# Six RMS norms of a hybrid decoder block: the factors computed per position on VectorE instead of per column with ScalarE's tables

## The chip, the cores and the metric

The kernel runs on one core of a Trainium2 chip. The time is device microseconds (us) of one execution of the whole program, weights and activations starting in device memory. A core has five engines, each with its own in-order queue of instructions: TensorE (PE in the profile, with its weight loads as PEld), VectorE (DVE), ScalarE (ACT), GpSimd (POOL) and SyncE (SP). Engines wait for one another only through semaphores, so an instruction that waits also holds back everything behind it on its own engine.

## The reference, cut to what matters

One decoder layer in float32 on 2048 positions with 1024 channels: a norm, two token mixers side by side, an output projection with a residual, a second norm, a SwiGLU feed-forward with a residual, and a final norm.

```python
def rmsnorm(x, g):
    y = x * lax.rsqrt(jnp.mean(x * x, axis=-1, keepdims=True) + 1e-6)
    return y * g

h = rmsnorm(x, norm1_g)
proj = h @ w_in                      # both mixers' inputs
o_gla = ...                          # chunked gated linear attention, per-head norm, gate
o_conv = c_b * causal_depthwise_conv(c_c * c_h, conv_w)
x = x + jnp.concatenate([o_gla, o_conv], -1) @ w_out
h2 = rmsnorm(x, norm2_g)             # rewritten by the change
x = x + (silu(h2 @ w_ffn_gate) * (h2 @ w_ffn_up)) @ w_ffn_down   # 1024 -> 2816 -> 1024
return rmsnorm(x, norm_f_g)          # rewritten for the first half of the positions
```

The quantity in question is the factor `rsqrt(mean(x*x) + eps)`: one number for each position, shared by its 1024 channels.

## The kernel before, in words

**Layout.** The positions are cut into four blocks of 512 (`PB`), and two blocks form a half. A block is held transposed: 128 channels on the partitions and 512 positions along the free axis, in `KD` = 8 such tiles for the 1024 channels. A norm therefore has to add over the partitions, and its factor has to be the same on all 128 partitions of a column.

**Products.** Every float32 operand is split into a high and a low part (`split`: L145 copies it on ScalarE with rounding, L146 subtracts on VectorE), and each product runs as three matmuls (`product_step`, L358, L359 and L360). A `unit` multiplies a 2x2 arrangement of tiles with seven products in place of eight, so it needs sums and differences of weights (L341 to L348 on GpSimd, the splits giving tiles `wq`) and collects results with a copy on ScalarE (L378) and adds on VectorE (L382, tile `c`). `out_proj` uses plain products (L776, L777, L779) in four groups for pairs of output tiles; each group ends with four adds `y<-y,mm` on VectorE (L801), a store and squares that go into `ssx0` and `ssx1`, the running sums of squares of the two blocks of a half (ScalarE squares, GpSimd adds).

**Stages.** Projections and mixers come first, until 600.1 us in the trace. Then `out_proj(0)` and `out_proj(1)` run, then for each half `ffn_up` (11 rounds of two units, the second multiplied in at L876) and `ffn_down`.

**The norms.** There are six that the change touches, two in each of three generators:
- `h2_first` (L807) makes the first half's normed operands while TensorE does `out_proj(1)`. It calls `column_rstd` (L159 on, its sum at L163) for each of its two blocks with a factor in SBUF, tile `rb2`, and then goes into `combine`, whose scalings `h<-h,sml,rb` are L482 on VectorE.
- `h2_ahead` (L846) makes the second half's operands while `ffn_up(0)` runs, with `psum_rstd` (sum at L170) and a factor in PSUM.
- `finish_later` (L949) does the final norm of the first half while the feed-forward of the second half runs: it loads the first half's result tile by tile (`y`), squares it, calls `psum_rstd`, loads the tiles again, scales them and stores them to the output (L965). It first calls `preload_act_table_set`.

In all of them `ones` (128x128) times the 128x512 sum of squares puts the total on every partition; `finish_rstd` (L173 on) then takes logarithm and exponential on ScalarE (L176, L177, each with its own table set where another function came in between), the mean on VectorE (L178) and one Newton step of three operations (`newton`, L154 to L157). The final norm of the second half, in `last_unit` (L968 on), calls `finish_rstd` itself.

**What sets the order.** The generators yield after each small step. `out_proj` takes steps of `h2_first` itself; elsewhere `tick()`, called after each product, steps the queue `background` on every second call and the generator in `ahead` on every fourth. The resulting program is then ordered on each engine by a planner (`TileContext` with `schedule_with_timeline_sim=True`), which estimates when each instruction can start. All transfers are issued by SyncE's queue. PSUM's eight banks are one pool (`ps`), from which totals, factors and products take theirs in turn.

Of the kernel before, what the change touches and what calls it, by code (L numbers as in the profile page):

```python
# [10 lines left out]
F32 = mybir.dt.float32  # L11
F32R = mybir.dt.float32r
U32 = mybir.dt.uint32
AF = mybir.ActivationFunctionType
ALU = mybir.AluOpType
PSUM = bass.MemoryType.PSUM
# [2 lines left out]
P = 128  # L19
D = 1024  # L20
# [4 lines left out]
PT = PB // P  # L25
# [5 lines left out]
EPS = 1e-6  # L31
# [16 lines left out]
def tile_hymba_block(ctx, tc, x, xt, win, wa, wgu, wout, wffn, wdown, wdown_first, small, out):  # L48
    nc = tc.nc
    act, dve, pool, pe = nc.scalar, nc.vector, nc.gpsimd, nc.tensor  # L50

    def pool_of(name, bufs, **kw):
        return ctx.enter_context(tc.tile_pool(name=name, bufs=bufs, **kw))

    const = pool_of("const", 1)
# [4 lines left out]
    tiny = pool_of("tiny", 2)  # L60
# [4 lines left out]
    mixer = mixing.enter_context(tc.tile_pool(name="mixer", bufs=1))  # L65
# [1 line left out]
    bx = [mixing.enter_context(tc.tile_pool(name="bx", bufs=11)), None]  # L67


    ident = mixer.tile([P, P], F32, name="ident")  # L70
    make_identity(nc, ident)
    ones = const.tile([P, P], F32, name="ones")
    dve.memset(ones[:], 1.0)
# [6 lines left out]
    one_t = ones[:, 0:1]  # L80
# [43 lines left out]
    def col(c):  # L124
        return sml[:, c : c + 1]

    def bank(name="mm"):
        return ps.tile([P, PB], F32, name=name, tag="mm")

    def tt(name):  # L130
        return tp.tile([P, PB], F32, name=name, tag="t")

    def bt(name, shape=(P, PB)):
        return bx[0].tile(list(shape), F32, name=name, tag="b")

    def load(dst, src):
        return nc.sync.dma_start(dst, src)

    def store(dst, src):
        return nc.sync.dma_start(dst, src)  # L140
# [3 lines left out]
    def split(src, hi, lo):  # L144
        last_hi[:] = [act.activation(hi, src, AF.Copy)]  # L145
        return dve.tensor_tensor(lo, src, hi.bitcast(F32), ALU.subtract)  # L146

    def rsqrt(y, v, l, y0):

        act.activation(l, v, AF.Ln)  # L150
        act.activation(y0, l, AF.Exp, scale=-0.5)
        newton(y, v, l, y0)

    def newton(y, v, l, y0):  # L154
        dve.tensor_tensor(l, y0, y0, ALU.mult)
        dve.scalar_tensor_tensor(l, l, -0.5, v, ALU.mult, ALU.mult)
        dve.scalar_tensor_tensor(y, l, 1.5, y0, ALU.add, ALU.mult)  # L157

    def column_rstd(ssq, n, rb=None):  # L159

        rb = ssq if rb is None else rb
        tot = bank("tot")
        pe.matmul(tot[:], ones[:], ssq[:], start=True, stop=True)  # L163
        finish_rstd(rb, tot, n)
        return rb

    def psum_rstd(ssq, n):

        tot, rb = bank("tot"), bank("rb_ps")
        pe.matmul(tot[:], ones[:], ssq[:], start=True, stop=True)  # L170
        finish_rstd(ssq, tot, n, rb)
        return rb

    def finish_rstd(v, tot, n, rb=None):
        l, y0 = bt("l"), bt("y0")
        act.activation(l[:], tot[:], AF.Ln, bias=eps[:], scale=1.0 / n)  # L176
        act.activation(y0[:], l[:], AF.Exp, scale=-0.5)  # L177
        dve.tensor_scalar(v[:], tot[:], 1.0 / n, EPS, ALU.mult, ALU.add)  # L178
        newton((v if rb is None else rb)[:], v[:], l[:], y0[:])
# [33 lines left out]
    def split_op(src):  # L213
        o = opp.tile([P, 2, PB], F32R, name="op", tag="op")
        split(src, o[:, 0, :], o[:, 1, :])
        return o
# [4 lines left out]
    def combine(src, g, rb, put):  # L221


        order = [kj for k in range(4) for kj in ((k, 0), (k, 1), (k + 4, 1), (k + 4, 0))]
        ahead = deque()

        def fetch():
            if order:
                k, j = order.pop(0)
                h = bt("h")  # L230
                load(h[:], src(k, j))
                ahead.append((k, j, h))

        def quad():
            k, j, h = ahead.popleft()
            fetch()
            return scaled(col(g + k), rb[j], h)

        fetch()
        fetch()  # L240
        for k in range(4):
            b11 = quad()
            put("B11", k, b11)
            yield
            b12, t1 = quad(), bt("t1")
            pool.tensor_tensor(t1[:], b12[:], b11[:], ALU.subtract)
            put("T1", k, t1)
            yield
            b22 = quad()
            pool.tensor_tensor(t1[:], b22[:], t1[:], ALU.subtract)  # L250
            put("T2", k, t1)
            yield
            pool.tensor_tensor(b12[:], b22[:], b12[:], ALU.subtract)
            put("T3", k, b12)
            yield
            b21 = quad()
            put("B21", k, b21)
            yield
            pool.tensor_tensor(t1[:], b21[:], t1[:], ALU.subtract)
            put("T4", k, t1)  # L260
            yield
            put("B22", k, b22)
            yield
# [98 lines left out]
    def unit(src, ops, into=None):  # L362
# [13 lines left out]
        def copied(name, o, at):  # L376
            t = tt(name) if into is None else into[at]
            act.activation(t[:], o[:], AF.Copy)  # L378
            return t
# [291 lines left out]
    def gla_scores(b, t, kq, kt, v, g):  # L671
# [6 lines left out]
        for e in range(2):  # L678
            dve.copy_predicated(smv[:, e], mask[:].bitcast(U32), sc[e][:])
        kt_ps = ps.tile([P, 2, P], F32, name="kt_ps", tag="mm")  # L680
# [71 lines left out]
    def sum_squares(ssq, y, first):  # L752
        if first:
            act.activation(ssq[:], y, AF.Square)
        else:
            q = tt("q")
            act.activation(q[:], y, AF.Square)  # L757
            pool.tensor_tensor(ssq[:], ssq[:], q[:], ALU.add)  # L758

    def build_mix(half):  # L760
        def pair(b, k):
            return load_pair(s_gla[b][:, k] if k < HEADS else s_mix[b][k - HEADS])

        return [[pair(2 * half + j, k) for j in range(2)] for k in range(KD)]
# [42 lines left out]
    def h2_first(ssq, ops):  # L807


        for _ in range(6):  # L810
            yield
        rb = []
        for j in range(2):
            rb.append(tiny.tile([P, PB], F32, name="rb2", tag="rb"))
            column_rstd(ssq[j], D, rb[j])
            yield

        def put(n, k, h):
            if n in LATER:
                store(s_h2[n][k][:], h[:])  # L820
            else:
                ops[n].append(split_op(h[:]))

        yield from combine(lambda k, j: s_x1[j][k][:], C_G2, rb, put)

    def h2_rest(ops):
        hs = deque()
        order = [(n, k) for n in LATER for k in range(4)]

        def fetch():  # L830
            if order:
                n, k = order.pop(0)
                h = bt("h")
                load(h[:], s_h2[n][k][:])
                hs.append((n, h))

        for _ in range(4):
            fetch()
        while hs:
            for _ in range(2):  # L840
                n, h = hs.popleft()
                ops[n].append(split_op(h[:]))
                fetch()
            yield

    def h2_ahead(ssq):  # L846


        rb = []
        for j in range(2):  # L850
            for _ in range(2):
                yield
            rb.append(psum_rstd(ssq[j], D))

        def put(n, k, h):
            store_split(s_h2p[n][k], h)

        yield from combine(lambda k, j: s_x1[2 + j][k][:], C_G2, rb, put)
# [34 lines left out]
    def store_split(dst, y):  # L893
        o = bx[1].tile([P, 2, PB], F32R, name="so", tag="so")
        split(y[:], o[:, 0, :], o[:, 1, :])
        store(dst[:], o[:].bitcast(F32))
# [6 lines left out]
    def ffn_down(half):  # L903
# [42 lines left out]
        if half == 0:  # L946
            ahead[:] = [finish_later(half)]

    def finish_later(half):  # L949

        for j in range(2):
            ssq = tiny.tile([P, PB], F32, name="ssx0", tag="ssx0", bufs=1)
            for d in range(KD):
                y = bt("y")
                load(y[:], s_x1[2 * half + j][d][:])
                yield
                sum_squares(ssq, y[:], d == 0)
            yield
            act.preload_act_table_set("natural_log_exp_and_others")
            rb = psum_rstd(ssq, D)  # L960
            for d in range(KD):
                y = bt("y")
                load(y[:], s_x1[2 * half + j][d][:])
                yield
                dve.scalar_tensor_tensor(y[:], y[:], col(C_GF + d), rb[:], ALU.mult, ALU.mult)  # L965
                store(out[2 * half + j, :, d, :], y[:])
# [73 lines left out]
    ssq = out_proj(0, build_mix(0))  # L1040
    drain_background(lambda: (3, PT - 1) in done)
    h2 = no_operands()
    ssq = out_proj(1, build_mix(1), h2_first(ssq, h2), h2_rest(h2))
    ahead.append(h2_ahead(ssq))
    mixing.close()
    bx[:] = [
# [112 lines left out]
```

## Time and profile before

| | |
|---|---|
| median of 3 runs | 2129.43 us (2121.35 to 2132.37) |
| profiled execution | 2130.55 us, span 2128.8 us |
| granted TensorE clock, mean | 0.987 |
| TensorE busy | 2043.5 us (96%), 9133 matmuls |
| VectorE busy | 1415.6 us (66%), 1983 instructions |
| ScalarE busy | 1015.7 us (48%), 1997 instructions |
| GpSimd busy | 971.7 us (46%), 703 instructions |
| DMA | 470.74 MB, 60.6% of 16 engines' time |

In the lines quoted below, a timeline row gives the start in us, the duration in us, the engine, the line of the kernel, the operation, the output and inputs by the program's names, the tile and the count; a row may stand for a few equal instructions in a row (x2, x4). A bracket at the end is the idle time of that engine just before the instruction, and what ended it. A row by groups gives the busy time of the group in us, the mean duration of one in ns, and the idle time before its instructions. A row by stretch gives the stretch, and then busy times with the number of instructions for PE, PEld, DVE, ACT and POOL, the granted clock, the DMA share and the traffic in GB/s.

### The profile page before, as it was taken

How to read it: one execution, taken by the hardware profiler on the slowest of the kernel's cores; microseconds unless marked ns; L12 is line 12 of the kernel's file. 1: busy time of each engine (PE TensorE's matmuls, PEld its weight loads, DVE VectorE, ACT ScalarE, POOL GpSimd, SP SyncE). 2: the span in 40 equal slices, each digit the busy share in tenths (PEclk: the TensorE clock that was granted, in tenths of full speed). 3: DMA queues.
4: the chain of work that ended last, by engine and by line, in shares of the span. 5: the costliest groups of instructions: out<-in, count | busy, mean ns of one | idle time of the engine just before them, and what ended most of it. 6: DMA issues, size and time to landing. Idle time of an engine off the chain costs nothing.

```text
span 2128.8 us, 26931 instructions
## 1 busy us (share of the span) xinstructions
PE 2043.5 (96%) x9133; PEld 1653.7 (78%) x9133; DVE 1415.6 (66%) x1983; ACT 1015.7 (48%) x1997; POOL 971.7 (46%) x703
## 2 busy tenths in 40 slices
PE   5999999999999999999999999999999989999996
PEld 4777787887888888788888877787888878886774
DVE  7668765549753695887886655654766666664554
ACT  5555445656543345545545443333554454453344
POOL 3435322222102464565464437864545545435774
PEclk9999999999999999999999999999999999999998
DMA  7349586424586872655646677697454535587662
GB/s 272 127 149 310 189 337 216 144 100 133 183 302 219 333 275 99 238 198 212 224 168 217 256 304 262 239 343 291 158 211 170 208 129 187 203 330 268 266 267 109
DMA packets 190971, 470.74 MB, mean 221 GB/s; under 512 B 20016, under 2 KB 65264, under 8 KB 181232
## 3 DMA queue, kind: packets, MB, share of 16 engines
q1 hardware_dynamic: 190832, 469.01, 60.6%
q8 instruction: 72, 1.18, 0.2%
q14 instruction: 67, 0.55, 0.1%
HBM read 300.63 MB, written 168.30 MB: 220 GB/s over the span
## 4 chain that ended last, share of the span: by engine, by line
PE 76%; DMA 10%; DVE 8%; ACT 3%; issue 2%; POOL 0%; SPq 0%; DVEq 0%; ACTq 0%; POOLq 0%
PE mm L358 22%; PE mm L360 22%; PE mm L359 21%; PE mm L776 2%; PE mm L777 2%; PE mm L779 2%; DMA raw<-in_wdown_dram 2%; DVE wq L146 2%; DMA op<-sa_T 1%; DMA op<-sa_B 1%; DMA op<-shT 1%; DVE so L146 1%; DVE op L146 1%; DMA h<-in_xt_dram 1%; DVE h L482 1%
## 5 line engine op out<-in xcount | busy, mean ns | idle before, releaser
L358 PE MATMUL mm<-op,wq 128*128 128x512 f32 x2499 | 985.4, 396 | 29.1 <-ACT c L378 9.8
L360 PE MATMUL mm<-op,wq 128*128 128x512 f32 x2499 | 970.4, 393 | 14.9 <-DVE wq L146 14.0
L359 PE MATMUL mm<-op,wq 128*128 128x512 f32 x2499 | 979.2, 392 | 0.0
L146 DVE TENSOR_TENSOR wq<-raw,wq 128x512 fp32r<-128x512 f32 (+2 forms) x626 | 524.6, 844 | 334.0 <-ACT wq L145 332.1
L145 ACT ACTIVATE wq<-raw 128x512 fp32r<-128x512 f32 (+2 forms) x626 | 364.8, 587 | 588.3 <-PE mm L360 421.2
L358 PEld LDWEIGHTS mm<-op,wq 128*128 128x128 f32 x2499 | 472.5, 189 | 147.8 <-ACT c L378 13.1
L360 PEld LDWEIGHTS mm<-op,wq 128*128 128x128 f32 x2499 | 472.5, 189 | 126.5 <-DVE wq L146 27.1
L359 PEld LDWEIGHTS mm<-op,wq 128*128 128x128 f32 x2499 | 472.9, 189 | 97.0 <-issue 1.0
L343 POOL TENSOR_TENSOR raw<-s,raw 128x512 f32<-128x512 f32 (+2 forms) x97 | 127.2, 1311 | 437.2 <-DVE wq L146 416.6
L382 DVE TENSOR_TENSOR c<-mm,c 128x512 f32<-128x512 f32 x267 | 182.8, 685 | 113.2 <-PE mm L360 109.9
L341 POOL TENSOR_TENSOR s<-raw 128x512 f32<-128x512 f32 (+2 forms) x97 | 127.3, 1313 | 196.5 <-DMA raw<-in_wffn_dram 90.3
L348 POOL TENSOR_TENSOR raw<-raw 128x512 f32<-128x512 f32 (+2 forms) x97 | 125.9, 1298 | 137.0 <-DVE wq L146 129.8
L378 ACT ACTIVATE c<-mm 128x512 f32<-128x512 f32 x267 | 154.4, 584 | 26.4 <-PE mm L360 23.9
L758 POOL TENSOR_TENSOR ssx<-ssx,q 128x512 f32<-128x512 f32 x52 | 76.2, 1477 | 159.8 <-ACT q L757 159.6
L342 POOL TENSOR_TENSOR raw<-raw 128x512 f32<-128x512 f32 (+2 forms) x97 | 136.8, 1411 | 4.4
L938 POOL TENSOR_TENSOR y<-c,y 128x512 f32<-128x512 f32 x66 | 99.1, 1504 | 68.9 <-DVE c L382 68.7
L146 DVE TENSOR_TENSOR so<-t,so 128x512 fp32r<-128x512 f32 x100 | 90.8, 914 | 19.0 <-ACT so L145 18.7
L145 ACT ACTIVATE wq<-s 128x512 fp32r<-128x512 f32 (+2 forms) x97 | 56.8, 586 | 92.7 <-PE mm L360 90.7
L776 PE MATMUL mm<-op,wq 128*128 128x512 f32 x256 | 100.9, 395 | 0.0
L777 PE MATMUL mm<-op,wq 128*128 128x512 f32 x256 | 99.8, 390 | 0.0
L146 DVE TENSOR_TENSOR wq<-s,wq 128x512 fp32r<-128x512 f32 (+2 forms) x97 | 86.1, 887 | 16.0 <-ACT wq L145 15.3
L145 ACT ACTIVATE so<-t 128x512 fp32r<-128x512 f32 x100 | 62.5, 628 | 44.2 <-DMA sa_B<-so 17.5
(175 smaller groups left out, 1882.2 us busy)
## 6 DMA issues: line engine op xcount, KB each, us to landing
raw<-in_wffn_dram SPq DMA_DIRECT2D x44, 1024.0 KB, 5.9
sa_T<-so SPq DMA_DIRECT2D x88, 512.0 KB, 5.0
op<-sa_T SPq DMA_DIRECT2D x88, 512.0 KB, 9.6
sa_B<-so SPq DMA_DIRECT2D x69, 512.0 KB, 3.4
op<-sa_B SPq DMA_DIRECT2D x69, 512.0 KB, 9.6
raw<-in_win_dram SPq DMA_DIRECT2D x23, 1024.0 KB, 5.3
raw<-in_wdown_dram SPq DMA_DIRECT2D x24, 768.0 KB, 6.1
sx<-y SPq DMA_DIRECT2D x48, 256.0 KB, 3.1
```

The source lines that it names most:

```text
L145: last_hi[:] = [act.activation(hi, src, AF.Copy)]
L146: return dve.tensor_tensor(lo, src, hi.bitcast(F32), ALU.subtract)
L341: pool.tensor_tensor(s1, a21, a22, ALU.add)
L342: pool.tensor_tensor(a21, a11, a21, ALU.subtract)
L343: pool.tensor_tensor(a11, s1, a11, ALU.subtract)
L358: pe.matmul(o[:], wh, xh, start=first and k == 0, stop=False, skip_group_check=True)
L359: pe.matmul(o[:], wh, xl, start=False, stop=False, skip_group_check=True)
L360: return pe.matmul(o[:], wl, xh, start=False, stop=k == n - 1, skip_group_check=True)
L378: act.activation(t[:], o[:], AF.Copy)
L382: dve.tensor_tensor(t[:], o[:], t[:], ALU.add)
L776: pe.matmul(o[e, j][:], wh, m[:, 0, :], start=k == 0, stop=False)
L777: pe.matmul(o[e, j][:], wh, m[:, 1, :], start=False, stop=False)
```

## The change

`column_rstd` and `psum_rstd` are replaced by `position_rstd`, in all three generators. The sum over partitions is now four matmuls with the 128x128 pieces of the sum of squares as weights and one column of ones as the moving operand. This puts the 512 totals into a 128x4 tile, positions on the partitions, in a PSUM bank `rs`. VectorE computes mean plus epsilon, takes a first guess of the reciprocal root by integer arithmetic on the bits of the number, and improves it in three Newton rounds of three operations, all on 128x4. It then copies each number along 128 columns into `rep` (128x4x128), and four transpositions on TensorE with `ident` put the factors, equal on all partitions, into the PSUM bank `rb_ps`. `h2_first` copies that to SBUF on ScalarE; the other two use it where it is. `ident` moves to a pool that lives to the end of the program, and `finish_later` no longer preloads a table set. `last_unit` is not changed.

```diff
--- before.py
+++ after.py
@@ -11,6 +11,7 @@
 F32 = mybir.dt.float32
 F32R = mybir.dt.float32r
 U32 = mybir.dt.uint32
+I32 = mybir.dt.int32
 AF = mybir.ActivationFunctionType
 ALU = mybir.AluOpType
 PSUM = bass.MemoryType.PSUM
@@ -67,7 +68,7 @@
     bx = [mixing.enter_context(tc.tile_pool(name="bx", bufs=11)), None]
 
 
-    ident = mixer.tile([P, P], F32, name="ident")
+    ident = const.tile([P, P], F32, name="ident")
     make_identity(nc, ident)
     ones = const.tile([P, P], F32, name="ones")
     dve.memset(ones[:], 1.0)
@@ -156,19 +157,29 @@
         dve.scalar_tensor_tensor(l, l, -0.5, v, ALU.mult, ALU.mult)
         dve.scalar_tensor_tensor(y, l, 1.5, y0, ALU.add, ALU.mult)
 
-    def column_rstd(ssq, n, rb=None):
-
-        rb = ssq if rb is None else rb
-        tot = bank("tot")
-        pe.matmul(tot[:], ones[:], ssq[:], start=True, stop=True)
-        finish_rstd(rb, tot, n)
-        return rb
-
-    def psum_rstd(ssq, n):
-
-        tot, rb = bank("tot"), bank("rb_ps")
-        pe.matmul(tot[:], ones[:], ssq[:], start=True, stop=True)
-        finish_rstd(ssq, tot, n, rb)
+    def position_rstd(ssq, n):
+
+
+
+        s, rb = bank("rs"), bank("rb_ps")
+        tot, v, l = [s[:, i * PT : (i + 1) * PT] for i in range(3)]
+        y = tiny.tile([P, PT], F32, name="py", tag="py")[:]
+        for t in range(PT):
+            pe.matmul(
+                tot[:, t : t + 1], ssq[:, t * P : (t + 1) * P], one_t, start=True, stop=True
+            )
+        dve.tensor_scalar(v, tot, 1.0 / n, EPS, ALU.mult, ALU.add)
+        li = l.bitcast(I32)
+        dve.tensor_scalar(li, v.bitcast(I32), 1, None, ALU.arith_shift_right)
+        dve.tensor_scalar(y.bitcast(I32), li, -1, 0x5F3759DF, ALU.mult, ALU.add)
+        for _ in range(3):
+            dve.tensor_tensor(l, v, y, ALU.mult)
+            dve.scalar_tensor_tensor(l, l, -0.5, y, ALU.mult, ALU.mult)
+            dve.scalar_tensor_tensor(y, l, 1.5, y, ALU.add, ALU.mult)
+        rep = bt("rep", (P, PT, P))
+        dve.tensor_copy(rep[:], y.rearrange("p (t c) -> p t c", c=1).to_broadcast([P, PT, P]))
+        for t in range(PT):
+            pe.transpose(rb[:, t * P : (t + 1) * P], rep[:, t, :], ident[:])
         return rb
 
     def finish_rstd(v, tot, n, rb=None):
@@ -812,7 +823,7 @@
         rb = []
         for j in range(2):
             rb.append(tiny.tile([P, PB], F32, name="rb2", tag="rb"))
-            column_rstd(ssq[j], D, rb[j])
+            act.activation(rb[j][:], position_rstd(ssq[j], D)[:], AF.Copy)
             yield
 
         def put(n, k, h):
@@ -850,7 +861,7 @@
         for j in range(2):
             for _ in range(2):
                 yield
-            rb.append(psum_rstd(ssq[j], D))
+            rb.append(position_rstd(ssq[j], D))
 
         def put(n, k, h):
             store_split(s_h2p[n][k], h)
@@ -956,8 +967,7 @@
                 yield
                 sum_squares(ssq, y[:], d == 0)
             yield
-            act.preload_act_table_set("natural_log_exp_and_others")
-            rb = psum_rstd(ssq, D)
+            rb = position_rstd(ssq, D)
             for d in range(KD):
                 y = bt("y")
                 load(y[:], s_x1[2 * half + j][d][:])
```

## The prediction

> **What bounds the kernel now.** I read the page's shares and its chain first, then the waits of TensorE, then the timeline around each of the six norms that the change rewrites.
>
> ```profile
> span 2128.8 us, 26931 instructions
> PE 2043.5 (96%) x9133; PEld 1653.7 (78%) x9133; DVE 1415.6 (66%) x1983; ACT 1015.7 (48%) x1997; POOL 971.7 (46%) x703
> PE 76%; DMA 10%; DVE 8%; ACT 3%; issue 2%; POOL 0%; SPq 0%; DVEq 0%; ACTq 0%; POOLq 0%
> PE mm L360 <- DVE wq L146: 14.0, 11, 2.5
> PE mm L358 <- DVE c L382: 7.7, 2, 7.0
> ```
>
> TensorE is busy for 96% of the span. A change can therefore move the time in three ways: through TensorE's own instructions, through waits that it puts into TensorE's in-order queue, or through waits that it removes. The two wait rows (total, times, longest) name the only large one in the feed-forward: 7.0 us behind one VectorE add. The profiled execution took 2130.55 us, 1.1 above the median of 2129.43; the sum below is made against 2130.55.
>
> **What ScalarE gives up.** In the built program the table loads fall from 29 to 17, and six Ln and six Exp go.
>
> ```profile
> L176 ACT ACT_TABLE_LOAD x4 | 5.1, 1283 | 0.1
> L176 ACT ACTIVATE l<-tot,eps 128x512 f32<-128x512 f32 x8 | 5.5, 684 | 1.6 <-PE tot L984 1.4 <-PE tot L163 0.2
> ```
>
> The 12 loads are 15.4 us and the pairs of activations 7.9 us, on an engine that is busy 48% of the time. By themselves they are worth nothing; they count only where VectorE or TensorE stood behind them.
>
> **TensorE's own instructions.** Each norm loses one product with `ones` over 512 columns and gains four over one column and four transpositions.
>
> ```profile
> 820.40 0.39 PE L360 MATMUL mm<-op,wq 128*128 128x512 f32 x1
> 820.62 1.02 PE L170 MATMUL tot<-ssx,ones 128*128 128x512 f32 x2
> 821.71 0.39 PE L359 MATMUL mm<-op,wq 128*128 128x512 f32 x1
> 387.49 0.39 PE L702 MATMUL o_ps<-carry,kq 128*128 128x128 f32 x2
> 387.71 0.39 PE L700 MATMUL o_ps<-vt,scores 128*128 128x128 f32 x2
> 362.28 0.60 PE L736 MATMUL ot<-ident,osb 128*128 128x128 f32 x4
> 362.95 0.39 PE L359 MATMUL mm<-op,wq 128*128 128x512 f32 x1
> ```
>
> Products start every 0.227 us (the first and last of the rows 715.03 to 725.72 further down are 47 products apart: 10.69 / 47). With the old sum away, L359 at 821.71 would follow the sum's place one step behind 820.62, at 820.85: the sum costs 0.86. Without the four transpositions L358 would start at 362.28 and L359 at 362.51; L359 starts at 362.95, so four cost 0.44. A one-column product in f32 is not in the trace. Its ends are 0.11 (one transposition) and 0.43 (half of the old sum). I take 0.22, the step between two f32 products of 128 columns (387.49 to 387.71), because with so few columns the loading of 128x128 weights sets the step. Four are 0.88. A norm costs 0.88 + 0.44 - 0.86 = +0.46 us, six cost **+2.8** (bounds +0.1 to +7.8).
>
> **VectorE's chain.** Twelve operations on 128x4 that wait for one another and a copy to 128x512 take the place of four operations on 128x512.
>
> ```profile
> 310.98 0.16 DVE L156 SCALAR_TENSOR_TENSOR hl<-hl,hsq 128x4 f32<-128x4 f32 x1
> 311.18 0.16 DVE L157 SCALAR_TENSOR_TENSOR hsq<-hl,hy 128x4 f32<-128x4 f32 x1
> 107.33 0.22 DVE L449 COPY rep<-msq 128x128 f32<-128x128 f32 x1
> 326.50 1.29 POOL L341 TENSOR_TENSOR s<-raw 128x512 f32<-128x512 f32 x1
> 326.94 0.87 DVE L155 TENSOR_TENSOR hl<-hy 128x4 f32<-128x4 f32 x1
> L876 DVE TENSOR_TENSOR c<-c,c 128x512 f32<-128x512 f32 x66 | 69.0, 1045 | 0.0
> L876 DVE TENSOR_TENSOR sg<-mm,sg 128x512 f32<-128x512 f32 x22 | 15.2, 691 | 55.6 <-PE mm L360 55.6
> ```
>
> A step is 0.20 us, so twelve take 2.4. The copy lies between 0.22 (128 columns) and 0.88 (four times that); I take 0.45. The chain is 2.85 us, about what four operations at 0.6 took. The last four rows show a hazard: the 128x4 operation at 326.94 lasts until GpSimd's add ends (327.79). The L876 rows show the same multiplication at 1045 ns with both inputs in SBUF and at 691 ns with one in PSUM. The new steps keep one operand in the PSUM tile `rs`, so I count no such holding for them, only for the copy. The Trainium skill (SBUF — State Buffer, section Who interferes with whom) says that a VectorE instruction with two SBUF inputs contends with GpSimd for an exclusive port pair, and one with a single SBUF input outside the two-port modes does not; by that rule, too, the steps run free, while a copy in a two-port mode can be held. If the steps were held after all, the sum would be the slower rival's.
>
> **The second norm in the second half's `out_proj`.** Here the built order matters. TensorE's queue has the sums of block 0, 37 products, four transpositions, the sums of block 1, the last 11 products of the first group, and then the transpositions of block 1. VectorE's queue has, inside the chain of block 1, the four adds `y<-y,mm` (L801) of that group, the last of which needs its last product, and one weight split behind them. The transpositions thus cannot start before the group's end plus all of that.
>
> ```profile
> 700.87 2.64 DVE L801 TENSOR_TENSOR y<-y,mm 128x512 f32<-128x512 f32 x4 [2.49 <-PE mm L779]
> 713.08 1.88 PE L163 MATMUL tot<-ssx,ones 128*128 128x512 f32 x4
> 715.03 0.39 PE L777 MATMUL mm<-op,wq 128*128 128x512 f32 x1
> 719.86 1.41 DVE L482 SCALAR_TENSOR_TENSOR h<-h,sml,rb 128x512 f32<-128x512 f32 x2
> 725.72 0.39 PE L776 MATMUL mm<-op,wq 128*128 128x512 f32 x1
> 861.58 0.50 PE L360 MATMUL mm<-op,wq 128*128 128x512 f32 x1 [2.51 <-DVE wq L146]
> 861.92 0.40 PE L358 MATMUL mm<-op,wq 128*128 128x512 f32 x1
> 1740.76 0.80 PE L358 MATMUL mm<-op,wq 128*128 128x512 f32 x1 [7.05 <-DVE c L382]
> 1744.31 0.40 PE L360 MATMUL mm<-op,wq 128*128 128x512 f32 x1
> ```
>
> Counted from the group's end (the next group's first product, 725.72 now, some 726.2 then): second add done at +0.3, two further adds 1.3, three steps between 0.6, the split 0.65, four steps 0.8, the copy 0.45, hand-over 0.3: TensorE idles about 4.4 us where it idled none (bounds 3.5 to 7). Slow products follow: after the 7.05 us wait eight of them take 3.55 us instead of 1.82, after the 2.51 us wait none is slow; I take 1.1 between 0 and 1.7. **+5.5**. The Trainium skill (TensorE: Matmul & The Clock Gate, section What's actually happening) puts the half clock after an idle window of some 3.4 us, which would make the slow stretch 1.7 and the term 6.1; the trace agrees at 7.05 us, and no run here has a 4 us wait.
>
> **What waits for it.** In `h2_first` VectorE's scaling (719.86) can begin only at 730.6, 10.7 later, less 2.6 for the four adds that it has then done: 8.1. TensorE itself is 0.5 + 4.4 + 0.5 + 1.1 = 6.5 late.
>
> ```profile
> 727.00:760.00 33.00, 33.00 (x148) 27.31 (x147) 32.85 (x34) 12.72 (x22) 24.83 (x16) 1.00 0.85 299
> 799.18 0.50 PE L360 MATMUL mm<-op,wq 128*128 128x512 f32 x1 [2.12 <-DVE wq L146]
> 764.85 1.11 DVE L146 TENSOR_TENSOR op<-t,op 128x512 fp32r<-128x512 f32 x1 [1.85 <-ACT op L145]
> ```
>
> In the first row (fourth number: VectorE busy) VectorE has no slack for 33 us, and at 799.18 TensorE already waits for it. So the 1.6 us by which VectorE falls further behind than TensorE would lengthen that wait, and gaps such as the 1.85 us at 764.85 may swallow it: **+0.8** (0 to 1.6).
>
> **Waits that go.** Around 843 to 852 VectorE waited on ScalarE's tables; around 1734 TensorE did, through it.
>
> ```profile
> 843.28 1.02 PE L170 MATMUL tot<-ssx,ones 128*128 128x512 f32 x2
> 848.14 0.69 DVE L178 TENSOR_SCALAR ssx<-tot 128x512 f32<-128x512 f32 x1 [3.26 <-ACT l L176]
> 851.90 0.74 DVE L482 SCALAR_TENSOR_TENSOR h<-h,sml,rb_ps 128x512 f32<-128x512 f32 x1
> 1734.52 0.68 DVE L146 TENSOR_TENSOR wq<-s,wq 128x512 fp32r<-128x512 f32 x1
> 1733.25 0.63 ACT L145 ACTIVATE so<-t 128x512 fp32r<-128x512 f32 x1 [1.27 <-DMA sa_B<-so]
> 1736.95 0.69 DVE L178 TENSOR_SCALAR ssx<-tot 128x512 f32<-128x512 f32 x1 [1.75 <-ACT l L176]
> 1740.02 0.68 DVE L382 TENSOR_TENSOR c<-mm,c 128x512 f32<-128x512 f32 x1
> ```
>
> In `h2_ahead` the second factor is ready at 843.28 + 0.88 + 24 products (5.45) + 0.44 = 850.05, so the scalings that began at 851.90 come 1.8 earlier; I take **-1.5** off the 2.51 us wait at 861.58 (0 to -2.5). In `finish_later` the add L382 that TensorE waits for stood in VectorE's queue behind L178 and L155, which waited for tables. It now follows the split of 1734.52 and one `so` split: about 1736.2 instead of 1740.02, 3.8 sooner. Twelve products later stand the transpositions, whose chain ends about 1740.4 while TensorE gets there between 1739.7 and 1741.3; this returns up to 0.7. **-3.0** (0 to -8.6, if the wait and its slow products went altogether). The other three norms have chains that end 1 to 5 us before their transpositions come up (37, 36 and 24 products at 0.227 behind the sums, against 2.85 and up to three 0.7 us operations): nothing; with that cover gone each costs what its chain is late. DMA issues keep their number (1245); the stores of `y` move ahead of some loads of `h` on SP, which no wait row of TensorE shows as short.
>
> **Sum**: 2.8 + 5.5 + 0.8 - 1.5 - 3.0 = +4.6, so 2135.2, given as **2135**, 0.3% above the median. About 0.5% (10.6 us) is what a measurement of this kernel can tell from no change.
>
> **Rivals.** *VectorE, not TensorE, sets when the feed-forward starts.* For it: the full 33 us and the wait at 799.18. Then its whole 8.1 us of delay arrives there in place of 5.5 + 0.8 and the first two norms' 0.9, and if GpSimd's two adds of squares hold the chain's steps (2 x 1.3), 10.7. With four norms' 1.9 and no gain at 861.58 or 1740 that is 2130.55 + 12.6 = **2143**. It decides once VectorE gains nothing on TensorE between 732 and 800; against it are ScalarE waits in that stretch that could shrink. *The removed waits go entirely* (-8.6 and -2.5) *and the new wait causes no slow products*: 2.8 + 4.4 - 11.1 = -3.9, **2127**; for it speaks that both waits stand behind tables alone, against it that at 1733.25 ScalarE also waited 1.27 us for a store. That the tables stay is excluded by the built program.
>
> **How the numbers follow.** 0.56 for the sum (2128 to 2140), 0.28 for the slower rival (2140 to 2150), 0.16 for the faster (2118 to 2128; the runs shown reach 2121.35 by themselves). The range 2122 to 2148 leaves out the outer parts of both rivals, some 0.06 at each end. Slower by over 0.5% needs 2140.1, which is the slower rival and the upper edge of the sum: 0.30. Faster by over 0.5% needs 2118.8, the outer half of the faster rival: 0.07. Between: 0.63.
>
> **What would show it.** In the changed profile: a wait of TensorE at the second set of transpositions in `out_proj`, ended by the copy `rep`, of 3.5 to 7 us; the wait for L382 near 1740 halved; the wait at 861 shorter; 128x4 steps at 0.16 us even beside GpSimd; transpositions of the other norms without waits. Wrong would be the forecast if steps are held to 1.2 us each, if the wait at the feed-forward's start passes 4 us, or if a rearranged queue opens a wait elsewhere.

## The result, and the profile after

The changed kernel takes 2135.59 us (median of 22 runs, 2130.89 to 2141.16) against 2128.93 for the kernel before (22 runs): a ratio of 1.0035, 95% interval 1.0026 to 1.0044. It is slower by 6.7 us by the medians and by 7.4 by the ratio, within what was forecast. Its profiled execution took 2140.87 us (span 2139.1), 5.3 above its own median. 4.7 us of that stand ahead of 707 us, where both programs are equal, so below stages are compared and not spans.

The page of the changed kernel and its waits of TensorE (total, times, longest):

```profile
span 2139.1 us, 27100 instructions
PE 2048.5 (96%) x9193; PEld 1660.7 (78%) x9193; DVE 1414.9 (66%) x2037; ACT 994.8 (47%) x1975; POOL 969.9 (45%) x703
PE mm L371 <- DVE wq L147: 15.3, 14, 3.5
PE rb_ps L182 <- DVE rep L180: 3.4, 1, 3.4
PE mm L369 <- DVE c L393: 2.6, 2, 1.9
```

VectorE's work is the same as before (1414.9 against 1415.6 us), ScalarE has 21 us less and TensorE 5 us more. The 7.0 us wait for the add `c` (now L393) is down to 1.9. A wait for `rep` at the transpositions is new, and the waits for weight splits `wq` have grown by 1.3 in total. So far this is what the prediction described. Where the time went is in the timeline around the second norm and at the feed-forward's start:

```profile
719.27 0.16 DVE L171 TENSOR_SCALAR rs<-rs 128x4 f32<-128x4 f32 x1
721.68 0.43 DVE L180 COPY rep<-py 128x512 f32<-128x512 f32 x1
728.47 0.17 DVE L171 TENSOR_SCALAR rs<-rs 128x4 f32<-128x4 f32 x1 [2.76 <-PE rs L168]
729.50 1.29 DVE L812 TENSOR_TENSOR y<-y,mm 128x512 f32<-128x512 f32 x2
732.68 2.82 POOL L769 TENSOR_TENSOR ssx<-ssx,q 128x512 f32<-128x512 f32 x2 [20.16 <-ACT q L768]
733.28 0.17 DVE L177 SCALAR_TENSOR_TENSOR rs<-rs,py 128x4 f32<-128x4 f32 x1
733.68 0.69 DVE L180 COPY rep<-py 128x512 f32<-128x512 f32 x1
734.43 0.66 PE L182 MATMUL rb_ps<-ident,rep 128*128 128x128 f32 x4 [3.35 <-DVE rep L180]
735.19 0.63 PE L788 MATMUL mm<-op,wq 128*128 128x512 f32 x1
738.57 0.39 PE L788 MATMUL mm<-op,wq 128*128 128x512 f32 x1
734.15 1.85 SPq L138 DMA_DIRECT2D h<-sx  x4
735.12 0.60 ACT L826 ACTIVATE rb<-rb_ps 128x512 f32<-128x512 f32 x1 [2.05 <-PE rb_ps L182]
739.46 2.19 DVE L493 SCALAR_TENSOR_TENSOR h<-h,sml,rb 128x512 f32<-128x512 f32 x3 [5.09 <-DMA h<-sx]
777.27 0.73 PE L790 MATMUL mm<-op,wq 128*128 128x512 f32 x2 [1.56 <-DVE wq L147]
813.89 0.80 PE L371 MATMUL mm<-op,wq 128*128 128x512 f32 x1 [3.49 <-DVE wq L147]
```

The steps on 128x4 take 0.15 to 0.17 us, also while GpSimd adds (733.28 beside 732.68), and the copy `rep` takes 0.43 beside an idle GpSimd, 0.69 beside a busy one. TensorE waits 3.35 us for the second transpositions (734.43), and the eight products behind them start 0.43 apart instead of 0.23. VectorE's first scaling, L493, then waits another 3.7 us after its factor is there (735.12 + 0.60), because the loads of `h` were issued at 734.15, behind four stores and three loads of `y`. TensorE waits for a split of weights at 777.27, which it did not before, and 3.49 us at 813.89, where the product of 799.18 waited 2.12 us before.

### The profile page after: what moved, and what is told of

Its sections match the earlier page's. It is cut to its first block, busy times and chain, and to the rows that moved or that the text cites. A ratio compares the mean times of both kernels' runs of the same rounds, so it can differ in the third digit from the quotient of the medians.

```text
span 2139.1 us, 27100 instructions
## 1 busy us (share of the span) xinstructions
PE 2048.5 (96%) x9193; PEld 1660.7 (78%) x9193; DVE 1414.9 (66%) x2037; ACT 994.8 (47%) x1975; POOL 969.9 (45%) x703
## 4 chain that ended last, share of the span: by engine, by line
PE 74%; DMA 9%; DVE 9%; issue 3%; ACT 2%; POOL 2%; SPq 1%; DVEq 0%; ACTq 0%; POOLq 0%
PE mm L369 22%; PE mm L371 21%; PE mm L370 21%; DVE wq L147 2%; DMA raw<-in_wdown_dram 2%; PE mm L787 2%; PE mm L788 2%; PE mm L790 2%; DMA op<-shT 1%; DVE h L493 1%; DVE so L147 1%; DVE op L147 1%; DMA op<-sa_B 1%; PE a_ps L551 1%; DMA op<-sa_T 1%
## 5 line engine op out<-in xcount | busy, mean ns | idle before, releaser
L393 DVE TENSOR_TENSOR c<-mm,c 128x512 f32<-128x512 f32 x267 | 183.0, 686 | 114.8 <-PE mm L371 112.9
```

The source lines that it names most:

```text
L393: dve.tensor_tensor(t[:], o[:], t[:], ALU.add)
```

## The experiments

To compare executions, I take the start of the same matmul in two traces; the matmuls outside the norms come in the same order in all of them. The table gives how much later (+) it comes than in the kernel before, less that difference at 707.6 us, where the programs are still equal. The marks are times in the trace of before: 737 is behind the second norm of `h2_first`, 786 the end of `out_proj`, 799 the feed-forward's first long wait (the product of 799.18), 804 a few us behind it, 866 and 904 behind `h2_ahead`'s norms, 1545 just behind the old sum of `finish_later`'s first norm, 1600 and 1752 behind its first and its second norm, 2105 near the end.

```
                            737   786   799   804   866   904  1545  1600  1752  2105   ratio (95% interval)
kernel before again (e11)   0.0   0.0   0.3   1.9   2.9   2.7   0.5   0.7   1.0  -2.3   0.9996 (0.9980-1.0012)
changed kernel              6.2   8.0  10.1  11.5   8.4  11.5  10.1  11.9   7.1   6.0   1.0035 (1.0026-1.0044)
h2_first alone (e1)         5.9   7.7  10.1  12.5  12.5  13.7  11.7  12.0  11.5   8.8   1.0053 (1.0039-1.0066)
all but h2_first (e2)       0.0   0.0  -0.6  -0.6  -3.7  -1.0  -2.4   0.1  -4.7  -5.4   0.9974 (0.9961-0.9987)
finish_later alone (e3)     0.0   0.0  -1.0  -1.0  -1.0   0.1  -1.1   0.9  -3.9  -5.3   0.9992 (0.9981-1.0003)
  once more (e9)            0.0   0.0   0.4   2.0   2.0   2.8   1.4   3.9  -0.9  -1.5   0.9989 (0.9977-1.0000)
h2_ahead alone (e7)         0.0   0.0  -0.8  -0.8  -3.9  -2.6  -5.5  -5.2  -5.6  -9.6   0.9972 (0.9959-0.9984)
  once more (e10)           0.0   0.0  -0.3   1.3  -1.8  -0.6  -4.8  -4.2  -5.3  -9.4   0.9969 (0.9959-0.9978)
norms at 4 steps (e4)       1.0   1.1   4.9   6.7   3.6   6.4   5.0   7.2   2.4   0.7   1.0012 (0.9998-1.0026)
both sums first (e5)        1.0   1.0   0.8   0.8  -2.3   0.2  -2.6  -0.8  -5.6  -7.4   0.9971 (0.9960-0.9983)
before, 10 steps (e6)       0.0   0.0   3.8   6.1   6.0   8.5   9.1   9.1   9.1   5.6   1.0026 (1.0017-1.0036)
four loads early (e8)       8.2   8.2  11.8  13.2  10.1  12.6  11.0  13.5   8.7   7.4   1.0037 (1.0024-1.0051)
h2_ahead, 2nd later (e12)   0.0   0.0  -0.8  -0.8  -3.9  -1.9  -1.7  -0.7  -5.6  -5.8   0.9960 (0.9946-0.9974)
```

The first row is the kernel before executed once more. Its drift, up to 2.2 us between neighbouring marks and 3.3 in the last stretch, is the limit of what one trace can tell. The 1.6 us between its marks 799 and 804 are slow products, of which more below.

### One site at a time

Theory A was that all of the loss is made in `h2_first` and none of it is absorbed; its rivals were the prediction's own terms, and absorption by waits that exist anyway. `column_rstd`, `psum_rstd` and the preload stay in the code where a site keeps them.

```diff
@@ only h2_first @@
-            rb.append(position_rstd(ssq[j], D))
+            rb.append(psum_rstd(ssq[j], D))
...
+            act.preload_act_table_set("natural_log_exp_and_others")
-            rb = position_rstd(ssq, D)
+            rb = psum_rstd(ssq, D)
```

> Only the two norms of h2_first are by positions; the other four are as in the kernel before. Theory A (by the sites in the two traces): the changed kernel loses 6.2 us in the second half's out_proj and 4.7 us more up to the feed-forward's first products, and nothing gives that back, so this kernel takes 2128.9 + 10.9 = 2140 us (2137 to 2142), more than the full change. Theory B (the prediction's own terms): 5.5 + 0.8 + 0.9 = 7.2, so 2136. Theory C (delay is absorbed by waits that exist anyway, the 2.5 us at 861.58 above all): 2128.9 + 10.9 - 2.5 = 2137 or less, and the wait near 861 is gone from the profile.

Measured 1.0053, or +11.3 us of 2127.2 (+8.3 to +14.0). By the ratio that is theory A's +10.9; theory B's 7.2 lies outside, and theory C's 8.4 at the edge. The medians alone (2136.87 against 2127.22, +9.65) lie between A and C. The trace decides against C: the wait of before near 861 is still there, so it absorbed nothing.

```profile
871.66 0.50 PE L386 MATMUL mm<-op,wq 128*128 128x512 f32 x1 [2.54 <-DVE wq L147]
```

```diff
@@ all but h2_first @@
-            act.activation(rb[j][:], position_rstd(ssq[j], D)[:], AF.Copy)
+            column_rstd(ssq[j], D, rb[j])
```

> h2_first keeps its two norms by columns with ScalarE's tables; the four norms of the feed-forward are by positions. Theory A (sites): 4.8 us won in finish_later, nothing in h2_ahead: 2124 us, faster than both kernels. Theory B (the prediction's terms): -1.5 - 3.0 + 1.9 for TensorE's own instructions = -2.6, so 2126.3. Theory C (the two profiles differ by 4.7 us before 700 us, where the programs are equal, so the late gain is no property of the change): 2129 to 2131.

Measured 0.9974, -5.5 us (-8.3 to -2.8): the four other norms make the kernel faster than before. That is nearest to theory A's 4.8; theory B's 2.6 lies at the edge. With the run above, +11.3 - 5.5 = +5.8 stands beside the +7.4 of the full change (1.0035 of 2128.93), which agrees within the intervals.

> Only finish_later's two norms are by positions. Theory A: the whole late gain of 4.8 us stands here, 2124 us, and the wait for the add L382 (7.05 us before) is under 2.5 us with no slow products behind it. Theory B: -3.0 + 0.9 = -2.1, 2127. Theory C: no change, 2129.

(The edit of the run before, and `h2_ahead` keeps `psum_rstd` too.) Measured 0.9992, -1.7 us, less than A's 4.8 and nearer to the prediction's 2.1, although the wait at the add fell as A said (the slow products behind it stayed). The same edit for `h2_ahead` in place of `finish_later`, and both once more, with a second trace of the kernel before:

> Only h2_ahead's two norms are by positions. Theory A (sites: the 2.5 us wait at 861.58 goes, but as much comes back near 900, where weight splits stand behind stores of the feed-forward): no change, ratio 0.9995 to 1.0005. Theory B (the difference of the medians of the runs with four and with two norms, 2122.7 and 2125.7, belongs to this site): -3 us, 0.9985. The prediction's terms: -1.5 + 0.9 = -0.6, 0.9997.

> The kernel with finish_later's two norms alone by positions, once more. Theory A (its trace: from the products at 1591 to those at 1742 it gains 5.4 us on the kernel before, as every kernel with this part does): the first measurement (0.9992, 0.9981 to 1.0003) was at the edge of its spread, and this one shows -3 to -5.5 us, 0.9974 to 0.9986. Theory D (what is won at 1742 is given back by TensorE's own waits later): again 0.999 to 1.000, and the trace loses 3 us or more behind 1742.

> The kernel with h2_ahead's two norms alone by positions, once more. The first measurement was 0.9972, its trace showed 2.2 us won up to 865, 1 us of it given back up to 903, and 5 us more up to 1741 in stretches where nothing is changed. Theory A (the site is worth 1 to 3 us, the rest is spread): 0.9985 to 0.9995. Theory B (it is worth 6 us, through the order of the transfers behind it): 0.997 again, and the trace again wins 3 us or more between 903 and 1741.

> The kernel before itself, for a second trace: how far two executions of the same program drift apart between the marks 707, 803, 903, 1591, 1742 and the end. Up to 1 us between neighbouring marks is what the readings by site assume; 3 us or more in the last stretch (1742 to the end) would mean that only the medians can speak for it.

`h2_ahead` alone measured 0.9972 and 0.9969 (-6 to -7 us), `finish_later` alone 0.9992 and 0.9989 (-2 us). In `finish_later` something is given back, as theory D said, but ahead of the gain and not behind it: from 1600 to 1752 all eight traces with its second norm by positions win 4.8 us, and from 1545 to 1600 the seven with the first one lose 1.8 to 2.6. Since 1545 lies behind the old sum, 0.6 us of this only balance what its removal wins just ahead of the mark: from 1540 to 1560 the seven lose 1.1 to 1.2 us. The timeline of the second trace of `finish_later` alone shows where:

```profile
1546.06 0.28 PE L168 MATMUL rs<-ones,ssx 128*128 128x1 f32 x2
1551.29 0.73 PE L168 MATMUL rs<-ones,ssx 128*128 128x1 f32 x6
1552.46 0.50 PE L384 MATMUL mm<-op,wq 128*128 128x512 f32 x1 [0.44 <-ACT c L404]
1594.42 0.50 PE L384 MATMUL mm<-op,wq 128*128 128x512 f32 x1 [0.42 <-ACT c L404]
1738.90 0.66 PE L384 MATMUL mm<-op,wq 128*128 128x512 f32 x1 [1.91 <-DVE c L408]
```

The sums of the first norm are split into one and three (each product shows as two matmuls), and two products behind wait 0.4 us each for ScalarE's copy `c`, besides the norm's own instructions. The second of these waits need not belong to the norm: the last kernel of this section has one there too, with the first norm by columns. In the last row the wait of 7.05 us is 1.91. For `h2_ahead`, the traces show the wait at 861 gone (-3.1 from 804 to 866 in both) and 1.3 of it given back by 904. The 2.9 and 4.3 us that they win between 904 and 1545 stand where nothing is changed, no single wait there explains them, and the kernel before itself drifts by 2.2 there. (For the 5 us that an expectation above gives for the first of them, this table has about 3.) The 6 us of theory B in the second run stand in two measurements, the traces show about 2 of them at the site, and the reason for the rest stays open.

The last kernel keeps what these runs favour: `h2_ahead` and only the second norm of `finish_later` by positions.

```diff
@@ all but h2_first, and: @@
-            rb = position_rstd(ssq, D)
+            if j == 0:
+                act.preload_act_table_set("natural_log_exp_and_others")
+                rb = psum_rstd(ssq, D)
+            else:
+                rb = position_rstd(ssq, D)
```

> h2_ahead's two norms and only the second norm of finish_later are by positions; h2_first and the first norm of finish_later stay by columns (with the preload of the tables for that one). By the marks in the traces, kernels with the first norm of finish_later by positions lose 2.0 to 2.6 us between 1545 and 1600, and those with the second win 4.8 to 5.3 between 1600 and 1752. Theory A (both marks belong to these two norms): 0.7 of the ratio 0.9971 of h2_ahead alone plus the second norm alone, that is -6.0 - 4.8 = -10.8 at best and -5.5 - 2.2 = -7.7 from the run with four norms: 2117 to 2120, ratios 0.995 to 0.9965. Theory D (gains of different sites do not add up): -5.5 to -6, 0.9972 to 0.9975.

Measured 0.9960 (0.9946 to 0.9974), the fastest kernel here: 8.5 us under the kernel before. The trace has -4.8 between 1600 and 1752 and still +0.9 ahead of it, with a wait for the copy `c` of its own:

```profile
1590.76 0.50 PE L384 MATMUL mm<-op,wq 128*128 128x512 f32 x1 [0.63 <-ACT c L404]
```

So theory A's claim that the loss ahead of 1600 belongs to the first norm holds only in part. The interval reaches theory D's 0.9974, so that it beats the kernel with four norms (0.9974) is likely and not shown.

### What `h2_first` loses

Two edits move its norms in the full change, one moves them in the kernel before.

```diff
@@ norms at 4 steps (e4) @@
-        for _ in range(6):
+        for _ in range(4):
@@ both sums first (e5), besides the line above @@
+        sums = [position_sums(ssq[j]) for j in range(2)]
         for j in range(2):
...
-            act.activation(rb[j][:], position_rstd(ssq[j], D)[:], AF.Copy)
+            act.activation(rb[j][:], position_factors(sums[j], D)[:], AF.Copy)
@@ kernel before, norms at 10 steps (e6) @@
-        for _ in range(6):
+        for _ in range(10):
```

(`position_sums` is the four products of `position_rstd`, `position_factors` the rest of it.)

> The full change, but h2_first begins its norms two steps earlier (4 in place of 6), so that the second norm's transpositions have 26 products in place of 11 between its sums and the group's end, and none of the four adds of the group stands inside its chain on VectorE; four loads of h are issued ahead of the stores of y in place of none. Theory A (the order around the group's end makes the loss): the 3.35 us wait at the transpositions and some 1.5 us of slow products go, and the feed-forward's start comes back to the kernel before's 2.1 us wait: 2135.6 - 4.9 - 3.7 = 2127. Theory B (VectorE's load, not the order, sets the feed-forward's start): only the first part goes, 2130.7. Theory C (the steps themselves cost it): 2135 to 2136.

Measured 1.0012, +2.5 us, so 4.9 of the loss are gone, as theory B said: the wait at the transpositions is away, and at 737 only 1.0 us is left for two norms' own instructions. But from `out_proj`'s end (1.1) the lateness still grows to 4.9 at 799, where the second execution of the kernel before has 0.3, and to 6.7 at 804. VectorE and TensorE in this kernel:

```profile
721.73 0.17 DVE L171 TENSOR_SCALAR rs<-rs 128x4 f32<-128x4 f32 x1 [4.80 <-PE rs L168]
727.39 0.75 DVE L493 SCALAR_TENSOR_TENSOR h<-h,sml,rb 128x512 f32<-128x512 f32 x1
801.21 0.51 PE L369 MATMUL mm<-op,wq 128*128 128x512 f32 x1 [2.17 <-ACT wq L146]
805.42 0.80 PE L371 MATMUL mm<-op,wq 128*128 128x512 f32 x1 [3.48 <-DVE wq L147]
```

VectorE idles 4.8 us because the second block's sums stand in TensorE's queue behind 34 products and the first transpositions, and it scales the first `h` at 727.39 (726.1 after taking off the 1.3 us that this trace is late at 707.6) instead of 719.86. What it does until the feed-forward does not make up for that.

> As the run with 4 steps (full change, norms of h2_first two steps earlier), but the sums of both blocks are issued next to each other, ahead of both chains, so that the second chain no longer waits for 34 products and the first transpositions; scalings can begin at about 717 us in place of 727. Theory V (the feed-forward's start is late by what VectorE's first scaling is late): the 5.5 us at 799 to 805 go, and only TensorE's own 0.9 us stay of h2_first: 2122.7 (the kernel with four norms changed) + 0.9 = 2123.6, at most 1.5 below, so a ratio of 0.998 to the kernel before. Theory W (what the two norms add in instructions sets it, wherever they stand): as the run with 4 steps, 1.001.

Measured 0.9971: theory V. With the same norms, steps and transpositions, and the sums side by side, the first scaling is at 720.59 (720.3 on the clock of before), and the lateness behind `out_proj` is gone (1.0 at 786, 0.8 at 799 and 804). The planner also moved transfers with it: six loads of `h` stand in a row ahead of the scaling, where the run with 4 steps has four, so the share of the loads is not measured apart. All six norms by positions are then as fast as four (0.9974).

```profile
720.59 2.08 DVE L500 SCALAR_TENSOR_TENSOR h<-h,sml,rb 128x512 f32<-128x512 f32 x3 [3.74 <-ACT rb L834]
800.34 0.50 PE L378 MATMUL mm<-op,wq 128*128 128x512 f32 x1 [1.99 <-DVE wq L147]
```

> The kernel before with none of the change, but h2_first begins its two norms two k-steps of out_proj later (10 steps in place of 6): 24 products, 5.5 us. Theory V: VectorE has no slack between its first scaling and the feed-forward, so the whole 5.5 us arrive there less a part of the four adds that it has then done (2.6): +3 to +5.5 us, a ratio of 1.0014 to 1.0026, and a wait of TensorE of 5 us or more near 800 in place of 2.1. The prediction's term (gaps swallow the delay): +0.8 us or less, 1.000 to 1.0004.

Measured 1.0026, +5.5 us (+3.6 to +7.7), the upper end of theory V, with no line of the change in it. In the trace the first scaling comes 5.3 us late (721.53 + 3.64 against 719.86), the product that waits at 799 is 3.8 late, and 804 is 6.1 late, behind slow products:

```profile
721.53 0.74 DVE L482 SCALAR_TENSOR_TENSOR h<-h,sml,rb 128x512 f32<-128x512 f32 x1
795.89 0.50 PE L358 MATMUL mm<-op,wq 128*128 128x512 f32 x1 [2.93 <-ACT wq L145]
799.37 0.79 PE L360 MATMUL mm<-op,wq 128*128 128x512 f32 x1 [2.75 <-DVE wq L146]
```

So most of a delay of VectorE's first scaling arrives at the feed-forward: 3.8 of 5.3 us at the product that waits, and the time agrees with all of it. One more run asked what the late loads of `h` have to do with it:

```diff
@@ four loads early (e8), in the full change @@
+        rest = combine(lambda k, j: s_x1[j][k][:], C_G2, rb, put, 4)
+        next(rest)
         for j in range(2):
...
-        yield from combine(lambda k, j: s_x1[j][k][:], C_G2, rb, put)
+        yield from rest
```

(With the 4, `combine` fetches four tiles and yields before its first scaling.)

> The full change, but the first four loads of h are issued before h2_first's norms, so the scaling does not wait for them (5.09 us at 739.46 in the changed kernel). In the built order two scalings and one split come to stand inside the second chain, so the wait at the transpositions should grow from 3.35 to about 5. Theory L (SyncE's order of loads behind the stores of y is a part of VectorE's delay): the feed-forward starts up to 3.7 us earlier, 2132 to 2133, a ratio of 1.0018 to 1.0025. Theory M (only the second factor counts, the loads are hidden behind it): 1.0035 or more.

Measured 1.0037: theory M, no gain. The loads were early and two tiles were scaled at 719.37, but those two and other work then stood inside the second chain, and the scaling went on only with the second factor:

```profile
719.37 1.41 DVE L495 SCALAR_TENSOR_TENSOR h<-h,sml,rb 128x512 f32<-128x512 f32 x2 [2.60 <-ACT rb L837]
727.19 1.12 PE L182 MATMUL rb_ps<-ident,rep 128*128 128x128 f32 x4 [5.06 <-DVE rep L180]
728.97 1.41 DVE L495 SCALAR_TENSOR_TENSOR h<-h,sml,rb 128x512 f32<-128x512 f32 x2 [1.84 <-ACT rb L837]
778.19 9.50 SPq L138 DMA_DIRECT2D y<-in_xt_dram  x4
795.34 0.63 ACT L146 ACTIVATE op<-h 128x512 fp32r<-128x512 f32 x1 [5.26 <-DMA h<-sfB]
```

The last two rows show a second way for the delay to arrive: SyncE's queue held four loads of `y` for 9.5 us, the reload of `h` behind them came late, and ScalarE waited 5.26 us for it. Since the edit changed both orders, what the late loads alone cost in the changed kernel stays open.

## Why the prediction was right, and where it was not

The time (2135 against 2135.59) was right, but partly by luck. Two errors cancelled, and the sum of +4.6 was set on a profiled execution 1.6 us above the median of before, while the change itself measured +6.7 by the medians and +7.4 by the ratio.

- **Own instructions**, +0.46 a norm: right. At 737 the kernels with moved norms are 1.0 us late for two norms.
- **VectorE's chain**, twelve steps of 0.2 and a copy of 0.45, not held by GpSimd: right. The first chain lasts from 719.27 to 722.11, 2.84 us. The rule of the Trainium skill that was quoted for it (SBUF — State Buffer, section Who interferes with whom) agrees with the trace: steps with an operand in PSUM ran at 0.17 beside GpSimd's add, and the copy was stretched to 0.69.
- **The wait at the second transpositions**, 4.4 us and 1.1 us of slow products, +5.5: the place and the cause were right, and the sum nearly (6.2 us at 737 with the norms' own instructions, against 6.4), with two parts off in opposite ways: 3.35 of wait, just under the bound of 3.5, and 1.6 of slow products. The wait was shorter because the second add ended at 730.79 (729.50 + 1.29), before the group did and not 0.3 behind it, and because the adds, the split and the steps between them overlapped. (That no run had a wait of 4 us overlooked one of 4.5 us for the last sum, L984; no stream of products follows it.)
- **"What waits for it", +0.8**: this step failed. It reckoned that VectorE falls only 1.6 us further behind than TensorE, and that gaps may swallow half of that. In the trace TensorE's lateness grows from 6.2 at 737 to 10.1 at 799 (1.6 of it in the new wait at 777.27, the prediction's own sign of a rearranged queue that opens a wait elsewhere) and, with slow products behind, to 11.5 at 804. VectorE's delay was under-sized, by the sentence that no wait showed the loads of `h` as short: the first scaling came 14.9 us late (739.46 against 719.86 + 4.66), not 10.7, with 3.7 of it behind those loads. The first rival had the mechanism, that VectorE's first scaling sets the feed-forward's start. That its price of 10.7 for this site is near the 11.3 of the ratio is luck: 2.6 of it stood for steps held by GpSimd, which were not held, and without them it said 8.1.
- **The wait at 861**, -1.5: it went altogether, as the faster rival had it, and the site is worth -6 by two measurements against -0.6 forecast (with the norms' own 0.9). More than about 2 us of that is not explained.
- **The wait for the add in `finish_later`**, -3.0: mis-sized, since the wait fell by 5.1, from 7.05 to 1.9 (-4.8 at the mark with the norm's own instructions in it). The add came 1.3 us behind the split ahead of it, where 1.7 was forecast and 5.5 had been, TensorE itself came a little later to the wait, and the chain behind the add returned nothing of the 0.7 that was taken off.

```profile
1736.86 0.68 DVE L147 TENSOR_TENSOR wq<-s,wq 128x512 fp32r<-128x512 f32 x1
1738.16 0.68 DVE L408 TENSOR_TENSOR c<-mm,c 128x512 f32<-128x512 f32 x1
```

- **"The other three norms: nothing"**: wrong by a little for the first norm of `finish_later`, which lost 1.1 to 1.2 us from 1540 to 1560, where its own instructions account for 0.5.

Together: +11.3 in `h2_first` where 7.2 was forecast, and -5.5 in the feed-forward where -2.6 was. The measurement told 0.35% from no change, with an interval of 0.1% to either side; the prediction had taken 0.5% as its limit.

## What to carry to other kernels

Moving a computation to another engine is judged by when its first consumer can start, not by its busy time: here one and the same set of instructions, begun at the same step, made the kernel 0.12% slower (no change lies just within the interval) or 0.29% faster, depending on whether two short sums stood together in TensorE's queue, and on what the planner moved with them. Where an engine shows next to no idle time between an event and a later stage, count most of the time by which the event moves as time of that stage (here 3.8 of 5.3 us at the wait, and 5.5 in the whole), and look for gaps in the rows of that engine. When two sites are changed, measure each by itself: a right total can hold two errors.

## What the runs showed of the hardware

TensorE's slow stretches, some eight products at 0.43 us in place of 0.23, do not follow from the length of the wait alone. In two executions of the kernel before, the same wait had different ends; rows of the one, and rows of the other (a row by stretch has the granted clock third from its end):

```profile
2065.38 0.80 PE L358 MATMUL mm<-op,wq 128*128 128x512 f32 x1 [2.58 <-ACT c L378]
2065.20:2068.40 3.20, 3.02 (x7) 2.44 (x8) 0.69 (x1) 1.22 (x3) 3.20 (x3) 0.50 0.72 242
861.58 0.50 PE L360 MATMUL mm<-op,wq 128*128 128x512 f32 x1 [2.51 <-DVE wq L146]
```

```profile
2062.86 0.50 PE L358 MATMUL mm<-op,wq 128*128 128x512 f32 x1 [2.58 <-ACT c L378]
2062.80:2066.00 3.20, 3.14 (x14) 2.61 (x15) 0.69 (x1) 1.87 (x5) 3.13 (x3) 1.00 0.73 244
861.82 0.50 PE L360 MATMUL mm<-op,wq 128*128 128x512 f32 x1 [2.55 <-DVE wq L146]
863.40 0.63 PE L360 MATMUL mm<-op,wq 128*128 128x512 f32 x1
```

Behind 2065.38 the next 16 starts took 1.6 us more than at full speed, and the granted clock was 0.50; behind 2062.86 they took 0.1 more, at a clock of 1.00. Behind 861.58 all products ran at full speed; in the second execution, after a wait of 2.55 us, they slowed only 1.3 us after TensorE had resumed. A shorter wait was enough too: in the first execution one of 1.53 us ended at 1936.93, with some of 0.3 to 0.4 us ahead of it, and from 1938.9 the clock was 0.50.

```profile
1936.93 0.50 PE L358 MATMUL mm<-op,wq 128*128 128x512 f32 x1 [1.53 <-ACT wq L145]
1938.90:1942.10 3.20, 3.20 (x9) 2.52 (x8) 1.65 (x3) 1.42 (x3) 2.22 (x2) 0.50 1.07 394
```

The prediction weighed the rule of the Trainium skill (TensorE: Matmul & The Clock Gate, section What's actually happening), by which the clock halves after an idle window of some 3.4 us and the windows run freely. That the outcome varies from run to run agrees with the free windows; that waits of 1.53, 2.55 and 2.58 us suffice does not agree with a window of 3.4 us that is idle throughout. A stretch of eight slow products is worth 1.6 to 1.7 us, a part of the spread between executions of one program.
